# Low parts of the retention's weights made beside the first FFN's down products and loaded later; the heads' normalization as one scale and bias on ScalarE

## The chip, the cores and the metric

The kernel runs on one core of one Trainium2 chip. The metric is the device time of one execution in microseconds (us), as the median of several runs. A trace of one execution gives the times of the instructions. TensorE (PE), VectorE (DVE), ScalarE (ACT), GpSimd (POOL) and SyncE (SP) each work their own queue of instructions in order; SP here only issues DMAs, and ACT and POOL issue some beside their other work.

## The reference

One block of a streaming encoder on 1024 frames of 1024 channels in f32: half a SwiGLU FFN, two token mixers on the same normalized input, a gated merge, a second half FFN, a gated embedding and a last norm.

```
h = h + 0.5 * swiglu(rms_norm(h, ffn1_norm), ffn1_w_gate, ffn1_w_up, ffn1_w_down)
u = rms_norm(h, mix_norm)
z = u @ w_in                     # q, k, v of attention, indexer and retention, and gates
aq, ak, av, iq, ik, iw, rq, rk, rv, rg, ga, gb = split(z)
y_a = dsa_attention(...)         # an indexer selects 256 keys of each query
y_r = group_norm_heads(retention(rope(rq), rope(rk), rv)) * silu(rg)
merged = sigmoid(ga) * (y_a @ w_branch_a) + sigmoid(gb) * (y_r @ w_branch_b)
h = h + merged @ w_out
h = h + 0.5 * swiglu(rms_norm(h, ffn2_norm), ...)

def group_norm_heads(y, g):      # per frame and head, over the head's 256 values
    mean = mean(y); var = mean((y - mean) ** 2)
    return (y - mean) * rsqrt(var + GN_EPS) * g
```

Retention has 4 heads with q and k of 128 and v of 256 channels each.

## The kernel before, in words

Every matrix product is made of three products of rounded factors: each f32 operand is split into a high part and a low part, and high by high, low by high and high by low are summed. A weight tile is 128 x 1024 values. For each, SP loads the raw tile (`wraw`), ACT copies it into the rounded type (`wh`, L144), and DVE or POOL subtracts to get the low part (`wl`, L146). The class `Weights` keeps the list of all tiles in the order in which they are used; four raw buffers and some seven pairs of `wh` and `wl` go round, so that loads and splits run ahead of their use. Whether DVE or POOL subtracts is an argument of each tile, `side`: POOL does it for the gate tiles, for the retention's heads and for `aq`.

PE's order is written out by hand (a manual schedule); the order on the other engines, and that in SP's queue, is set by the framework's scheduler from the program's text and its own costs. A semaphore between engines is waited for where a tile is shared.

The stages that matter here, by the trace:

- The first FFN's gate and up products end at about 503 us. Its weights are combined into seven products of the Strassen-Winograd kind, by POOL and DVE.
- The down products, 503 to 719 us: seven runs (A11, A12, S2, S1, S3, S4, A22, in this order), each over the same loop of 11 weight tiles (`NJ2`). A tile is 4 x 3 products of 128x512 with its own left and right half as factors (L683); half of a tile's values is an activation that POOL spilled before (`hf`), half is the weight. Only the last run has work between its tiles (`between`: the norm and the transposes of the mixers' input).
- Small products, the indexer's products and its scores, 719 to 880 us.
- The retention, some 880 to 1326 us: 32 units, one for each head and block of 128 frames. The weights of a head are four tiles `("r", h)`, 16 in all, and the gates' tiles are used in between (16 x 3 products of a gate tile into `pgate`, L1058, ACT then writes `gt`, L1065, which goes to DRAM, `gspill`). In a unit: q, k and v products (`prod`), the rope, the scores, the state's update (`sf`, `sh`, `sl`), the cross part (`y`, L1256, on ACT), then in `ret_values` the sum of both parts and the normalization (`bs`, `mv`, `y`, L1264 to L1274), and the transposed result times the gate.
- Through the first 19 or so of these units the attention's selection runs beside on DVE and ACT: 31 times, six blocks are compared with a candidate. For four of them DVE writes a mask (`bias`, L1124, 1024, 896, 768 and 640 columns) and ACT sums it (L1125), for two DVE does both (`eq`, L1127); then `hit`, `thr`, `cand`.
- Attention follows to 1548 us, the merge to 1710, and the second FFN, which is like the first.

Of the kernel before, what the change touches and what calls it, by code (L numbers as in the profile page):

```python
# [20 lines left out]
P = 128  # L21
# [67 lines left out]
class Weights:  # L89
# [3 lines left out]
    def __init__(self, nc):  # L93
        self.nc = nc
        self.raw_free, self.free, self.half_open = [], [], None
        self.loads, self.fills, self.pair, self.rows = [], [], {}, {}
        self.loaded = self.filled = 0
        self.limit = 0
        self.dropped = []

    def add(self, pool, raws=0, pairs=0):
        t = [pool.tile([P, 1024], F32, name=f"wraw{i}") for i in range(raws)]
# [45 lines left out]
    def plain(self, key, k, c, side, pieces):  # L148

        n = k * c  # L150

        def load(t):
            v = t[:, :n].rearrange("p (k c) -> p k c", k=k)
            for c0, c1, ap in pieces:
                self.nc.sync.dma_start(v[:, :, c0:c1], ap)

        at = self.new_load(1, load)

        def fill(slot, _):
            self.split(slot.h[:, :n], slot.l[:, :n], self.raw(at)[:, :n], side)  # L160
            self.used(at)
            return [(key, tuple(x[:, :n].rearrange("p (k c) -> p k c", k=k) for x in (slot.h, slot.l)))]

        self.fills.append(([at], False, 1, fill))
        self.rows[key] = k

    def matrix(self, key, top, bottom):

# [109 lines left out]
def hybrid_block_kernel(  # L278
# [14 lines left out]
    def krows(w, c0, c1, k0, k1):  # L293
        return w.rearrange("(k p) c -> p k c", p=P)[:, k0:k1, c0:c1]
# [55 lines left out]
    AQ, AK, IQ, IK, RQ, RK, RV, RG, GA, GB = 0, 512, 640, 1152, 1224, 1736, 2248, 3272, 4296, 5320  # L350
    TILES = [(RG, f) for f in range(8)] + [(c, f) for f in range(8) for c in (GB, GA)]

    def gate_jobs(n0, n1):
        for c, f in TILES[n0:n1]:
            c0 = c + f * P
            W.plain((c, f), KT, P, True, [(0, P, krows(w_in0, c0, c0 + P, 0, KT))])

    for i in range(2):
        group_jobs(("pp", i), w_ple_proj[0], [(512 * i, 512 * i + 512)], nk=2)
# [4 lines left out]
    gate_jobs(0, at_tile)  # L364
    for h in range(RH):
        group_jobs(("r", h), w_in0, [(RQ + P * h, RQ + P * h + P), (RK + P * h, RK + P * h + P),
                                     (RV + 256 * h, RV + 256 * h + 256)], side=True)
        gate_jobs(at_tile, at_tile + N_RET[h])
        at_tile += N_RET[h]
    group_jobs("aq", w_in0, [(AQ, AQ + 512)], side=True)  # L370
    gate_jobs(at_tile, len(TILES))
# [17 lines left out]
    def tok(b):  # L389
        return slice(b * P, (b + 1) * P)  # L390
# [93 lines left out]
    class Seven:  # L484
# [175 lines left out]
                gp.dma_start(wsp[self.name][j][:, :, 256 * q:256 * q + 256],  # L660
                             wd[q].rearrange("p f i c -> p (f i) c"))

        def down(self, hres, residual, finished, turn, other={}):
            bank_plan(mm=3, m1=1, dn=4)
            sums = [bank(t, "pda") for t in ("mm", "mm", "mm", "m1")]

# [8 lines left out]
            def run(a, ps, start, stop, between=None, load=None):  # L675
                for j in range(NJ2):
                    key = self.name, a, j
                    h, l = (x[:, 0] for x in W[key])
                    if load and j == 4:
                        load(h)  # L680
                    for i in range(4):
                        for n, (x_, y_) in enumerate(split3(h[:, tok(i)], l[:, tok(i)], h[:, 512:D], l[:, 512:D])):
                            nc.tensor.matmul(ps[i], x_, y_, start=start and j == 0 and n == 0,  # L683
                                             stop=stop and j == NJ2 - 1 and n == 2, skip_group_check=True)
                    W.release(key)
                    if between and between.get(j):
                        between[j]()

# [193 lines left out]
            f()  # L882

    finished = normed(mix_norm[0], hres, hspill)
    seven.down(hres, lambda b, i: x0[tok(b), half(i)], finished, turn, {4: lambda: W.drop(raws)})
    for b in range(2):
        for j in range(2):
            sm_product(2 * b + j, "dn")
# [369 lines left out]
    def ret_values(n):  # L1258
# [12 lines left out]
        nc.vector.bn_aggr(mv[:, 0:2], bs)  # L1271
        nc.vector.tensor_scalar(mv[:, 2:3], mv[:, 1:2], GN_EPS, None, op0=OP.add)
        nc.gpsimd.tensor_tensor(mv[:, 3:4], mv[:, 2:3], mhalf, op=OP.pow)
        nc.vector.tensor_scalar(y, y, mv[:, 0:1], mv[:, 3:4], op0=OP.subtract, op1=OP.mult)  # L1274
        R[n, "z"] = y

    def ret_store(n):
# [396 lines left out]
```

## Time and profile before

| | |
|---|---|
| median of 3 runs | 2575.51 us (2575.15 to 2577.4) |
| the profiled execution | 2573.51 us |
| its span in the trace | 2571.7 us |
| PE busy | 2467.5 us (96% of the span) |
| DVE busy | 1619.0 us (63%) |
| ACT busy | 1104.6 us (43%) |
| POOL busy | 1011.3 us (39%) |
| PE's granted clock, mean of the span | 0.986 |
| DMA | 349.34 MB, mean 136 GB/s |

The span is the time from the first to the last instruction of the trace; the profiled execution's own time is 1.8 us more. Busy times of different engines overlap. The clock is in shares of PE's full speed.

### The profile page before, as it was taken

The page shows a single profiled execution, that of the slowest core. Times are in us where ns is not written, and L with a number is a line of the kernel's source. Part 1 is how long each engine was busy: PE and PEld are TensorE (multiplying, and loading weights), DVE is VectorE, ACT ScalarE, POOL GpSimd, SP SyncE. Part 2 cuts the span into 40 slices and gives each one's busy share as a digit, 9 for nine tenths or more (in the row PEclk, how much of TensorE's full clock was granted, in tenths as well). Part 3 has the DMA queues.
Part 4 walks back from the last instruction along what each step waited for, and adds up shares of the span by engine and source line. Part 5 has one row for each costly group of instructions (what it writes and reads, how often), then busy time and mean ns, then how long its engine had stood idle before and what let it go on. Part 6 is the DMA issues. An engine that isn't in the chain of part 4 may idle for free.

```text
span 2571.7 us, 32603 instructions
## 1 busy us (share of the span) xinstructions
PE 2467.5 (96%) x11464; PEld 2016.4 (78%) x11464; DVE 1619.0 (63%) x2640; ACT 1104.6 (43%) x1900; POOL 1011.3 (39%) x934
## 2 busy tenths in 40 slices
PE   6999999999999989889999999999899999999998
PEld 5788877878887877667878887787688788878887
DVE  5555556575667889997457774644556665555564
ACT  5333333343445666652245663423433333333442
POOL 5667668400011343343343431003676686520000
PEclk9999999999999999999999999999999999999999
DMA  6345444586621222222221227653254444587622
GB/s 204 121 141 172 156 143 164 178 272 210 217 83 35 77 62 59 59 72 60 72 82 38 77 64 223 190 168 103 90 172 156 144 164 145 175 278 225 193 94 95
DMA packets 262052, 349.34 MB, mean 136 GB/s; under 512 B 20864, under 2 KB 172672, under 8 KB 259072
## 3 DMA queue, kind: packets, MB, share of 16 engines
q1 hardware_dynamic: 239264, 267.03, 34.2%
q0 software_dynamic: 15712, 67.64, 6.8%
q10 hardware_dynamic: 6912, 12.59, 1.3%
q8 instruction: 90, 1.47, 0.2%
q14 instruction: 74, 0.61, 0.1%
HBM read 246.00 MB, written 101.19 MB: 135 GB/s over the span
## 4 chain that ended last, share of the span: by engine, by line
PE 72%; DVE 13%; issue 5%; ACT 4%; POOL 3%; DMA 3%; SPq 0%; ACTq 0%; POOLq 0%; DVEq 0%
PE pa L566 18%; PE pc L566 13%; PE prod L440 10%; PE pda L683 9%; PE pdc L683 7%; PE pgate L1058 5%; PE pmrg L396 4%; DVE bias L1124 3%; DVE wl L146 1%; ACT bias L1125 1%; PE psc L396 1%; PE ppv L1388 1%; PE ppt L1377 1%; PE plg L396 1%; ACT wh L144 1%
## 5 line engine op out<-in xcount | busy, mean ns | idle before, releaser
L146 DVE TENSOR_TENSOR wl<-wraw,wh 128x1024 fp32r<-128x1024 f32 (+2 forms) x422 | 621.6, 1476 | 406.6 <-ACT wh L144 402.1
L144 ACT ACTIVATE wh<-wraw 128x1024 fp32r<-128x1024 f32 (+1 forms) x466 | 435.9, 937 | 759.4 <-PE pc L566 184.3
L440 PE MATMUL prod<-wh,uh 128*128 128x512 f32 (+1 forms) x648 | 266.0, 411 | 0.2 <-ACT gt L1065 0.2
L440 PE MATMUL prod<-wh,ul 128*128 128x512 f32 (+1 forms) x648 | 256.8, 396 | 0.0
L440 PE MATMUL prod<-wl,uh 128*128 128x512 f32 (+1 forms) x648 | 256.4, 396 | 0.0
L1058 PE MATMUL pgate<-uh,wh 128*128 128x512 f32 x384 | 158.9, 414 | 23.2 <-ACT gt L1065 22.3
L1058 PE MATMUL pgate<-uh,wl 128*128 128x512 f32 x384 | 153.8, 401 | 0.0
L1058 PE MATMUL pgate<-ul,wh 128*128 128x512 f32 x384 | 153.7, 400 | 0.0
L440 PEld LDWEIGHTS prod<-wh,ul 128*128 128x128 f32 x648 | 123.1, 190 | 29.0
L146 POOL TENSOR_TENSOR wl<-wraw,wh 128x1024 fp32r<-128x1024 f32 x44 | 108.9, 2478 | 91.5 <-ACT wh L144 91.0
L566 PE MATMUL pa<-uh,wh 128*128 128x512 f32 x352 | 141.2, 401 | 2.5 <-DVE ev L581 2.5
L1125 ACT ACTIVATE bias<-bias 128x1024 bf16<-128x1024 bf16 (+3 forms) x132 | 117.1, 888 | 59.0 <-DVE bias L1124 55.1
L683 PE MATMUL pda<-wh 128*128 128x512 f32 x352 | 138.7, 394 | 3.8 <-ACT wh L144 3.8
L566 PE MATMUL pa<-ul,wh 128*128 128x512 f32 x352 | 139.9, 398 | 1.5 <-DVE ul L403 1.5
L566 PE MATMUL pa<-uh,wl 128*128 128x512 f32 x352 | 139.7, 397 | 0.0
L566 PE MATMUL pc<-uh,wl 128*128 128x512 f32 x352 | 139.4, 396 | 0.0
L566 PE MATMUL pc<-ul,wh 128*128 128x512 f32 x352 | 139.3, 396 | 0.0
L683 PE MATMUL pda<-wl,wh 128*128 128x512 f32 x352 | 137.8, 391 | 1.5 <-DVE wl L146 1.5
L566 PE MATMUL pa<-th,wl 128*128 128x512 f32 x352 | 139.2, 395 | 0.0
L566 PE MATMUL pc<-uh,wh 128*128 128x512 f32 x352 | 139.2, 395 | 0.0
L566 PE MATMUL pa<-tl,wh 128*128 128x512 f32 x352 | 138.9, 395 | 0.0
L440 PEld LDWEIGHTS prod<-wh,uh 128*128 128x128 f32 x648 | 124.1, 191 | 18.5 <-ACT gt L1065 0.4
(280 smaller groups left out, 6000.6 us busy)
## 6 DMA issues: line engine op xcount, KB each, us to landing
wraw<-hf SPq DMA_DIRECT2D x154, 256.0 KB, 3.3
wraw<-in_ffn_w_gate_dram SPq DMA_DIRECT2D x44, 512.0 KB, 4.0
wraw<-in_ffn_w_up_dram SPq DMA_DIRECT2D x44, 512.0 KB, 3.9
wd<-in_ffn_w_down_dram SPq DMA_DIRECT2D x88, 256.0 KB, 4.3
wf<-wd POOLq DMA_DIRECT2D x44, 512.0 KB, 3.3
hf<-g POOLq DMA_DIRECT2D x22, 1024.0 KB, 5.6
wraw<-wf SPq DMA_DIRECT2D x88, 256.0 KB, 3.7
wraw<-in_ffn_w_down_dram SPq DMA_DIRECT2D x66, 256.0 KB, 3.9
```

The costliest lines, as they stand in the source:

```text
L144: self.nc.scalar.activation(h, src, AF.Copy)
L146: eng.tensor_tensor(l, src, h.bitcast(F32), op=OP.subtract)
L396: nc.tensor.matmul(ps, a, b, start=i == 0, stop=i == n - 1)
L440: nc.tensor.matmul(box[0][:, :cols], a, w, start=k == 0 and i == 0, stop=k == nk - 1 and i == 2)
L566: nc.tensor.matmul(ps, x_, y_, start=start and k == 0 and i == 0, stop=stop and k == 3 and i == 2, skip_group_check=True)
L683: nc.tensor.matmul(ps[i], x_, y_, start=start and j == 0 and n == 0, stop=stop and j == NJ2 - 1 and n == 2, skip_group_check=True)
L1058: nc.tensor.matmul(box[0], a, m, start=k == 0 and j == 0, stop=k == KT - 1 and j == 2)
L1124: nc.vector.tensor_scalar(m, x_, t[:, j:j + 1], None, op0=op)
L1125: nc.scalar.activation(m, m, AF.Copy, accum_out=cnt[:, j:j + 1])
L1377: nc.tensor.transpose(ps[:, (t - t0) * P:(t - t0 + 1) * P], L[:, t * P:(t + 1) * P], ident)
L1388: nc.tensor.matmul(pv[:, j].rearrange("p a c -> p (a c)"), vhl[:, s], pT[:, t].rearrange("p a c -> p (a c)"), start=s == 0, stop=s == b)
```

## The change

Two things are changed.

1. For 24 weight tiles (the 16 of the retention's heads and the 8 gate tiles that are used among them) the low part is made in the first FFN's down stage. `Weights.make`, called after tiles 1, 3, 5, 7 and 9 of each run that has nothing else between its tiles, loads up to three of these tiles ahead by SP into `lraw` (three buffers), makes the high part on ACT (`lh`), subtracts on POOL in place, and has POOL's queue write the result to DRAM (`low`). With five calls to a run, the 24 calls fall in A11, A12, S2, S1 and S3. In the retention ACT makes `wh` as before, and `wl` is loaded by a DMA on ACT's queue from `low`; POOL's subtraction of these 24 tiles is gone. The first gate tiles, `aq` and the later gates are as before.
2. In `ret_values`, y times `mv[3]` plus (minus mean times `mv[3]`) on ACT takes the place of DVE's subtraction and multiplication, with one more one-column operation on DVE for the bias.

```diff
--- before.py
+++ after.py
@@ -97,6 +97,23 @@
         self.loaded = self.filled = 0
         self.limit = 0
         self.dropped = []
+        self.to_make, self.making, self.made = [], [], {}
+
+    def make(self, pool, dram):
+
+        while self.to_make and len(self.making) < 3:
+            key, load = self.to_make.pop(0)
+            raw = pool.tile([P, 1024], F32, name="lraw", tag="lraw", bufs=3)
+            load(raw)
+            self.making.append((key, raw))
+        if not self.making:
+            return
+        key, raw = self.making.pop(0)
+        h = pool.tile([P, 1024], F32R, name="lh", tag="lh", bufs=2)
+        self.nc.scalar.activation(h, raw, AF.Copy)
+        self.nc.gpsimd.tensor_tensor(raw.bitcast(F32R), raw, h.bitcast(F32), op=OP.subtract)
+        self.made[key] = dram.tile([P, 1024], F32, name=f"low{len(self.made)}")
+        self.nc.gpsimd.dma_start(self.made[key], raw)
 
     def add(self, pool, raws=0, pairs=0):
         t = [pool.tile([P, 1024], F32, name=f"wraw{i}") for i in range(raws)]
@@ -157,12 +174,18 @@
         at = self.new_load(1, load)
 
         def fill(slot, _):
-            self.split(slot.h[:, :n], slot.l[:, :n], self.raw(at)[:, :n], side)
+            if side == "made":
+                self.nc.scalar.activation(slot.h, self.raw(at), AF.Copy)
+                self.nc.scalar.dma_start(slot.l.bitcast(F32), self.made[key])
+            else:
+                self.split(slot.h[:, :n], slot.l[:, :n], self.raw(at)[:, :n], side)
             self.used(at)
             return [(key, tuple(x[:, :n].rearrange("p (k c) -> p k c", k=k) for x in (slot.h, slot.l)))]
 
         self.fills.append(([at], False, 1, fill))
         self.rows[key] = k
+        if side == "made":
+            self.to_make.append((key, load))
 
     def matrix(self, key, top, bottom):
 
@@ -350,10 +373,10 @@
     AQ, AK, IQ, IK, RQ, RK, RV, RG, GA, GB = 0, 512, 640, 1152, 1224, 1736, 2248, 3272, 4296, 5320
     TILES = [(RG, f) for f in range(8)] + [(c, f) for f in range(8) for c in (GB, GA)]
 
-    def gate_jobs(n0, n1):
+    def gate_jobs(n0, n1, side=True):
         for c, f in TILES[n0:n1]:
             c0 = c + f * P
-            W.plain((c, f), KT, P, True, [(0, P, krows(w_in0, c0, c0 + P, 0, KT))])
+            W.plain((c, f), KT, P, side, [(0, P, krows(w_in0, c0, c0 + P, 0, KT))])
 
     for i in range(2):
         group_jobs(("pp", i), w_ple_proj[0], [(512 * i, 512 * i + 512)], nk=2)
@@ -364,8 +387,8 @@
     gate_jobs(0, at_tile)
     for h in range(RH):
         group_jobs(("r", h), w_in0, [(RQ + P * h, RQ + P * h + P), (RK + P * h, RK + P * h + P),
-                                     (RV + 256 * h, RV + 256 * h + 256)], side=True)
-        gate_jobs(at_tile, at_tile + N_RET[h])
+                                     (RV + 256 * h, RV + 256 * h + 256)], side="made")
+        gate_jobs(at_tile, at_tile + N_RET[h], "made")
         at_tile += N_RET[h]
     group_jobs("aq", w_in0, [(AQ, AQ + 512)], side=True)
     gate_jobs(at_tile, len(TILES))
@@ -660,7 +683,7 @@
                 gp.dma_start(wsp[self.name][j][:, :, 256 * q:256 * q + 256],
                              wd[q].rearrange("p f i c -> p (f i) c"))
 
-        def down(self, hres, residual, finished, turn, other={}):
+        def down(self, hres, residual, finished, turn, other={}, beside=lambda: None):
             bank_plan(mm=3, m1=1, dn=4)
             sums = [bank(t, "pda") for t in ("mm", "mm", "mm", "m1")]
 
@@ -683,6 +706,8 @@
                             nc.tensor.matmul(ps[i], x_, y_, start=start and j == 0 and n == 0,
                                              stop=stop and j == NJ2 - 1 and n == 2, skip_group_check=True)
                     W.release(key)
+                    if j % 2 and not between:
+                        beside()
                     if between and between.get(j):
                         between[j]()
 
@@ -882,7 +907,8 @@
             f()
 
     finished = normed(mix_norm[0], hres, hspill)
-    seven.down(hres, lambda b, i: x0[tok(b), half(i)], finished, turn, {4: lambda: W.drop(raws)})
+    seven.down(hres, lambda b, i: x0[tok(b), half(i)], finished, turn, {4: lambda: W.drop(raws)},
+               lambda: W.make(rt_pool, dram))
     for b in range(2):
         for j in range(2):
             sm_product(2 * b + j, "dn")
@@ -1271,7 +1297,8 @@
         nc.vector.bn_aggr(mv[:, 0:2], bs)
         nc.vector.tensor_scalar(mv[:, 2:3], mv[:, 1:2], GN_EPS, None, op0=OP.add)
         nc.gpsimd.tensor_tensor(mv[:, 3:4], mv[:, 2:3], mhalf, op=OP.pow)
-        nc.vector.tensor_scalar(y, y, mv[:, 0:1], mv[:, 3:4], op0=OP.subtract, op1=OP.mult)
+        nc.vector.scalar_tensor_tensor(mv[:, 2:3], mv[:, 0:1], -1.0, mv[:, 3:4], op0=OP.mult, op1=OP.mult)
+        nc.scalar.activation(y, y, AF.Identity, bias=mv[:, 2:3], scale=mv[:, 3:4])
         R[n, "z"] = y
 
     def ret_store(n):
```

POOL's queue in the first FFN's down products. `hres` are the tiny copies that a run makes at its tile 4, `hf` the last of the spilled activations; before:

```order
L635 DMA hf_85<-g_638 128x2048
L637 DMA hf_85<-s_3497 128x512
L671 COPY hres<-wh_3521 128x1 x4
L671 COPY hres<-wh_71 128x1 x4
L671 COPY hres<-wh_73 128x1 x4
L671 COPY hres<-wh_69 128x1 x4
L466 TENSOR_TENSOR nst<-nst,mhalf 128x1 x8
```

After, with the subtractions and writes (`lraw`, `low`) among them:

```order
L658 DMA hf_85<-g_638 128x2048
L660 DMA hf_85<-s_3497 128x512
L114 TENSOR_TENSOR lraw<-lraw,lh 128x1024 x2
L116 DMA low_3663<-lraw 128x1024
L116 DMA low_3704<-lraw 128x1024
L694 COPY hres<-wh_3521 128x1 x4
L114 TENSOR_TENSOR lraw<-lraw,lh 128x1024
L116 DMA low_3751<-lraw 128x1024
L114 TENSOR_TENSOR lraw<-lraw,lh 128x1024
L116 DMA low_3790<-lraw 128x1024
L694 COPY hres<-wh_71 128x1 x4
```

All 24 subtractions and their writes stand between the copies of the runs; the rows shown are those of the first two.

SP's queue for the first run, A11; `hf` is the activation half of a tile, `in_ffn_w_down` the weight half. Before:

```order
L155 DMA wraw_136<-hf_79 128x512
L155 DMA wraw_136<-in_ffn_w_down_dram 128x512
L155 DMA wraw_135<-hf_80 128x512
L155 DMA wraw_135<-in_ffn_w_down_dram 128x512
L155 DMA wraw_65<-hf_81 128x512
L155 DMA wraw_65<-in_ffn_w_down_dram 128x512
```

After, at the same tiles (in brackets the semaphores that a load waits for: DMAHW of DMAs on SP's queue, DMASW of DMAs on POOL's, DVE and Pool of those engines):

```order
L172 DMA wraw_136<-hf_79 128x512 [waits DMAHW1_49,DVE_49]
L172 DMA wraw_136<-in_ffn_w_down_dram 128x512 [waits DMAHW2_49]
L172 DMA lraw<-in_w_in_dram 128x8x128 [waits DMAHW3_49,DMASW0_49]
L172 DMA wraw_135<-hf_80 128x512 [waits DMAHW4_49,DVE_49]
L172 DMA wraw_135<-in_ffn_w_down_dram 128x512 [waits DMAHW5_49]
L172 DMA wraw_65<-hf_81 128x512 [waits DMAHW6_49,DVE_49]
L172 DMA wraw_65<-in_ffn_w_down_dram 128x512 [waits DMAHW7_49]
L172 DMA lraw<-in_w_in_dram 128x8x128 [waits DMAHW0_49,DMASW1_49,Pool_49]
L172 DMA wraw_66<-hf_82 128x512 [waits DMAHW1_49,DVE_49]
L172 DMA wraw_66<-in_ffn_w_down_dram 128x512 [waits DMAHW2_49]
```

The loads of `lraw` (one of 8 pieces of 128 columns for a gate tile, three for a tile of the heads) stand between the loads of the weights that follow, and wait for POOL's subtraction and for the write of the tile that had the buffer before. Ahead of the load of the last tile of S3 there are 22 tiles' worth of them.

ACT's queue at a head's change in the retention, before: `bias` are the sums of the selection, `wh` the high parts.

```order
L144 ACTIVATE wh_3523<-wraw_66 128x1024
L1125 ACTIVATE bias,cnt<-bias 128x1024
L144 ACTIVATE wh_69<-wraw_65 128x1024
L1125 ACTIVATE bias,cnt<-bias 128x896
L1125 ACTIVATE bias,cnt<-bias 128x768
L1223 ACTIVATE sts<-stf 128x128
L1125 ACTIVATE bias,cnt<-bias 128x640
L1242 ACTIVATE sh<-sf 128x256
L144 ACTIVATE wh_73<-wraw_66 128x1024
L1256 ACTIVATE y<-pc,cs 128x256
L402 ACTIVATE qkt<-pqkt 128x256
```

After, at the same unit; `wl` from `low` are the DMAs that ACT issues, and L1301 is the new activation.

```order
L179 DMA wl_3524<-low_3986 128x1024
L178 ACTIVATE wh_3523<-wraw_66 128x1024
L178 ACTIVATE wh_69<-wraw_65 128x1024
L1301 ACTIVATE y<-y,mv 128x256
L179 DMA wl_70<-low_4025 128x1024
L1249 ACTIVATE sts<-stf 128x128
L1268 ACTIVATE sh<-sf 128x256
L179 DMA wl_74<-low_4064 128x1024
L178 ACTIVATE wh_73<-wraw_66 128x1024
L1282 ACTIVATE y<-pc,cs 128x256
L425 ACTIVATE qkt<-pqkt 128x256
L1235 ACTIVATE kd<-qk,cs 128x128
```

The sums of the selection that stood among these rows stand elsewhere, each `wh` has a DMA beside it, the rows of `y` are new, and `kd` stands behind `qkt`. Over the whole, the selection had 9 of its iterations ahead of the first unit's rope and its last in unit 18 or so; it now has 7 and its last in unit 21.

## Rows read from the trace of the kernel before

**Rows 1.** Windows: stretch, then busy us (instructions) by engine, clock, DMA share, GB/s.

```profile
core 0: us, PE busy (x) PEld busy (x) DVE busy (x) ACT busy (x) POOL busy (x), PEclk, DMA share, GB/s
...
503.00:635.00 132.00, 129.48 (x570) 106.55 (x570) 83.91 (x102) 54.57 (x56) 14.42 (x23) 1.00 0.76 244
520.00:570.00 50.00, 50.00 (x222) 41.41 (x221) 40.76 (x64) 24.21 (x27) 2.29 (x8) 1.00 0.84 270
2270.00:2300.00 30.00, 30.00 (x133) 24.76 (x133) 18.96 (x18) 14.86 (x14) 1.60 (x4) 1.00 0.94 317
920.00:1200.00 280.00, 246.67 (x1130) 197.94 (x1129) 257.14 (x661) 160.35 (x365) 105.11 (x101) 0.93 0.20 59
1200.00:1326.00 126.00, 124.57 (x634) 103.43 (x634) 64.12 (x184) 41.15 (x87) 53.72 (x57) 1.00 0.29 83
```

**Rows 2.** Waits of PE, 720 to 1330 us: total, times, longest.

```profile
PE pgate L1058 <- ACT gt L1065: 22.3, 10, 4.7
```

**Rows 3.** The `bs` of the units: with the selection, and after it.

```profile
L1270 DVE BATCH_NORM_STATS2 bs<-y x18: 395/414/420, 965.2 to 1179.7; 128x6 f32<-128x256 f32 x18
...
L1270 DVE BATCH_NORM_STATS2 bs<-y x9: 414/419/428, 1242.9 to 1322.6; 128x6 f32<-128x256 f32 x9
```

**Rows 4.** Timelines of DVE, then of POOL, 1023 to 1037 us.

```profile
1023.82 2.49 DVE L1124 TENSOR_SCALAR bias<-sc,cand 128x896 bf16<-128x896 f32 x1
...
1028.89 2.38 DVE L1124 TENSOR_SCALAR bias<-sc,cand 128x640 bf16<-128x640 f32 x1
...
1033.10 0.41 DVE L1274 TENSOR_SCALAR y<-y,mv 128x256 f32<-128x256 f32 x1 [0.43 <-POOL mv L1273]
...
1034.12 1.54 DVE L1124 TENSOR_SCALAR bias<-sc,cand 128x1024 bf16<-128x1024 f32 x2
...
1035.91 1.07 DVE L1124 TENSOR_SCALAR bias<-sc,cand 128x768 bf16<-128x768 f32 x2
...
1023.17 2.67 POOL L146 TENSOR_TENSOR wl<-wraw,wh 128x1024 fp32r<-128x1024 f32 x1
...
1028.53 2.39 POOL L146 TENSOR_TENSOR wl<-wraw,wh 128x1024 fp32r<-128x1024 f32 x1
```

**Rows 5.** Groups of instructions, 920 to 1210 us: busy us, mean ns, idle before.

```profile
L1125 ACT ACTIVATE bias<-bias 128x768 bf16<-128x768 bf16 (+1 forms) x110 | 97.4, 886 | 45.5 <-DVE bias L1124 41.5 <-DVE mv L1271 3.4
L1124 DVE TENSOR_SCALAR bias<-sc,cand 128x1024 bf16<-128x1024 f32 (+1 forms) x108 | 92.6, 886 | 0.7
...
L146 POOL TENSOR_TENSOR wl<-wraw,wh 128x1024 fp32r<-128x1024 f32 x15 | 38.5, 2570 | 11.9 <-ACT wh L144 11.6
...
L1274 DVE TENSOR_SCALAR y<-y,mv 128x256 f32<-128x256 f32 x20 | 12.4, 619 | 9.4 <-POOL mv L1273 9.4
...
L1256 ACT ACTIVATE y<-pc,cs 128x256 f32<-128x256 f32 x18 | 8.3, 459 | 2.8 <-PE pc L396 2.8
...
L1272 DVE TENSOR_SCALAR mv<-mv 128x1 f32<-128x1 f32 x20 | 2.9, 144 | 0.0
```

**Rows 6.** Timelines of ACT and of PE at a gate product.

```profile
1040.39 0.58 ACT L1065 ACTIVATE gt<-pgate 128x512 f32<-128x512 f32 x1
...
1041.03 0.79 PE L1058 MATMUL pgate<-uh,wh 128*128 128x512 f32 x1 [4.71 <-ACT gt L1065]
```

**Rows 7.** The page's DMA issues: KB each, us to landing.

```profile
wf<-wd POOLq DMA_DIRECT2D x44, 512.0 KB, 3.3
```

**Rows 8.** DVE's groups by form, 60 to 500 us.

```profile
L146 DVE TENSOR_TENSOR wl<-wraw,wh 128x1024 fp32r<-128x1024 f32 x44 | 77.5, 1761 | 71.6 <-ACT wh L144 71.6
```

**Rows 9.** Timelines of SP's queue, DVE and PE at tile 54.

```profile
630.92 0.32 SPq L155 DMA_DIRECT2D wraw<-hf  x1
...
640.54 1.23 DVE L146 TENSOR_TENSOR wl<-wraw,wh 128x1024 fp32r<-128x1024 f32 x1 [1.50 <-ACT wh L144]
...
652.40 0.39 PE L683 MATMUL pda<-wl,wh 128*128 128x512 f32 x1
```

**Rows 10.** DMA of 503 to 635 us in 40 equal slices.

```profile
GB/s 153 220 348 271 299 281 280 181 252 395 245 264 379 125 237 281 315 255 291 274 330 274 220 212 166 182 204 227 263 254 334 233 222 166 169 186 225 194 179 179
```

## The prediction

> **What bounds the kernel now.** I read the busy times by stretch first [rows 1]. PE carries nearly the whole span, so only a stage in which PE waits can give much, and a stage in which it never waits can only lose; these rows show which is which. In the down products of the first FFN (503 to 635 us) PE works 129.5 of 132 us at a clock of 1.00: nothing to gain there. In the retention with the selection (920 to 1200 us) it works 246.7 of 280 us at a granted clock of 0.93, while DVE works 257.1 of 280, or 92%. After the selection (1200 to 1326 us) PE is back at 124.6 of 126 us and clock 1.00, with DVE half idle. So the stage that the change aims at is bound by DVE and by what waits for DVE, not by PE.
>
> The wait list of PE over 720 to 1330 us [rows 2] has as its largest entry the gate product waiting for ACT's `gt`: ten times, 22.3 us. ACT is 57% busy there; `gt` comes late because ACT works in order, and counts and casts that themselves wait for DVE stand ahead of it (ACT's `bias` sums waited 41.5 us for DVE's `bias`, in the first row of [rows 5]). The `bs`, one for each unit, give the pace [rows 3]: 965.2 to 1179.7 us in 17 steps, 12.62 us a unit, with the selection; 1242.9 to 1322.6 us in 8 steps, 9.96 us, without it.
>
> Why DVE is so full shows in its timeline beside POOL's [rows 4]. A count over 128x1024 takes 0.77 us (two in 1.54) when POOL does no subtraction. But `bias` of 128x896 took 2.49 us from 1023.82 and `bias` of 128x640 2.38 us from 1028.89; each lies on a POOL `wl` of 2.4 to 2.7 us (1023.17 and 1028.53). `bias` reads one tensor and is held for almost the whole of POOL's instruction.
>
> **The change, part by part.**
>
> *Removed from the retention: 24 POOL subtractions, 15 of them in 920 to 1210 us (38.5 us of POOL)* [rows 5]. POOL's own time is worth nothing, it waits most of the time. What counts is DVE's held time. 108 `bias` counts take 92.6 us, mean 886 ns. Undisturbed ones are 0.77 us for 1024 columns and 0.54 for 768 (two in 1.07); over the four sizes (mean 832 columns) that is about 0.6, and I take 0.65. The excess is 108 x 0.236 = 25.5 us. `y` has a mean of 619 ns against 0.41 undisturbed (1033.10): 20 x 0.21 = 4.2 us.
>
> *Moved from DVE to ACT: the normalization of a head.* DVE loses `y` (20 x 0.41 = 8.2 us) and gets a one-column operation, which by the other one-column operation on `mv` (144 ns) costs 20 x 0.144 = 2.9 us. ACT gets a 128x256 activation, which by its own `y` of that shape takes 459 ns, 20 x 0.46 = 9.2 us; it is 57% busy, and the place that the activation has ahead of `sts` delays that by half a microsecond, less than what the unit gains. Nothing is charged for it; were ACT full, it would be 9 us.
>
> DVE's saving in the stage is then 25.5 + 4.2 + 8.2 - 2.9 = 35 us in some 20 units. DVE is 92% busy, so I count 92% of it as time of the stage: **32 us**. The bounds: at most every unit runs at the free pace, 19 x 2.66 = 50 us; at least DVE's certain saving without the stalls, 20 x 0.619 - 2.9, about 10 us, if the blocked time lay beside other waits. In the order PE's gate products keep their place, and the ACT rows around `v` and `kd` move by a place or two, so I take the value nearest to the engine that is full.
>
> *Added to the retention: 24 loads of a low part from DRAM, issued by ACT.* An issue took SP 0.32 us (at 630.92 [rows 9]); by that 15 are 5 us of ACT's queue, which has 120 us of idle time. The load of a weight half waits for the same slot as ACT's `wh` does. 512 KB from POOL's queue lands 3.3 us after issue [rows 7], against ACT's `wh` and then POOL's `wl` of 2.6 us before, and the DMA is 20% busy in this stage: nothing.
>
> *Added to the down products: 24 tiles' worth of loading, splitting and writing.* ACT gets 24 `lh` copies, at the mean of its instructions there (54.57 us in 56) 1 us each, and is 54.6 of 132 us busy. POOL gets 24 x 2.5 and is 14.4 of 132 busy. Both hide it. DVE's `wl` of 128x1024 took 1.23 us at 640.54 [rows 9], and 1.76 on the mean in 60 to 500 us, beside POOL's work on the FFN [rows 8]; five POOL subtractions of 2.5 us a run of 30 us make POOL 42% busy, so perhaps 0.3 us on each of 11 tiles, 3 us of a run in which a tile's low part is ready 11 us ahead of its use (tile 54: DVE ends at 641.77, PE starts at about 652.4 [rows 9]). Only in the first run, where that lead is not yet built, do I charge **3 us** (0 to 6).
>
> The DMA is what has no slack. In 503 to 635 us the kernel moves 244 GB/s, in 132 us 32.2 MB, and the engines are 76% busy [rows 1]. In SP's queue 22 of the new loads stand ahead of the load of tile 54 (the last one of S3), which SP issues at 630.92 [rows 9]; the first three stand ahead of the first run's loads and can go before 503 us. With about 20 writes of low parts by then, 39 x 0.524 = 20.4 MB come on top: 52.7 MB. To be there in time the load must have landed ACT's and DVE's 2.3 us before PE's start, by about 650, so the 52.7 MB have 147.5 us, 357 GB/s. What rate is there? The best stretch that I found, 2270 to 2300 us, moves 317 GB/s at 94% DMA share; 520 to 570 us moves 270 at 84%; single slices of 3.3 us reach 395 [rows 1, 10]. At 317 the last byte comes at 503 + 166.2 = 669.2 us, **19 us late**. At 270 it is 698, 48 late; at 395 it is on time. I take 317: the stretch is long and near full. SP's wait for the low write of three tiles before (a loop of load, `lh`, subtraction 2.5 and a write, 3.3 + 1 + 2.5 + 3.3 or about 10 us at the landing time of [rows 7], in three turns of two tiles each, 16 us) does not bind unless the DMA does; if it does, the weight loads queued behind that wait on SP come late, and PE with them, which is the same 19 us and not one more.
>
> The Trainium skill's page "DMA: Bandwidth & Descriptors", section "Where 436 GB/s comes from", puts the limit of HBM for one core at about 358 GB/s. By that figure 52.7 MB take 147.2 us and the load is on time, and the sum would be 19 us less; no long stretch of this trace reaches it, and the 94% stretch, scaled to full, is at 337.
>
> The sum: -32 + 19 + 3 = **-10 us** on the profiled 2573.5 us, which is 2 us under the median of the runs, 2575.5. On the median's scale: **2565.5 us**.
>
> **The rivals.**
>
> *B, the transfers fit.* DMA packets of the added loads fill the gaps of a 76% busy stage, at the rate of the peak slices; then the delay is 0 and the time 2575.5 - 32 + 3 = 2546.5. For it: slices of 395 and 379 GB/s. Against it: none lasts longer than 3.3 us. The skill's 358 GB/s would give this time too.
>
> *C, the other side: the transfers become the bound of the down products.* The added loads come in pieces of 512 bytes and 1 KB, and writes share the engines. At the 270 GB/s of 520 to 570 us the tile comes 48 us late: 2575.5 - 32 + 48 + 3 = 2594.5. It decides below the rate at which the delay eats the gain of 29: 52.7 MB in 176.5 us, 299 GB/s. For it: 84% DMA share at 270 GB/s, so the share and the rate don't rise together. Against it: 94% at 317.
>
> *D, the stage keeps its pace.* PE waits there for ACT's `gt`, and ACT's order is fixed; if its head is a count that waits for another thing, DVE's freed time becomes idle time. The gain is then 10: 2575.5 - 10 + 22 = 2587.5. For it: `gt` at 1040.39 is followed by a PE that had stood 4.71 us [rows 6], and the wait list names ACT and not DVE. Against it: 41.5 of the 45.5 us that ACT's sums waited are DVE's.
>
> *E, nothing.* Gain and loss cancel within 5 us: 2575.5.
>
> **Chances and range.** Forecast .45 (its own range 2548 to 2582), B .20, C .15, D .15, E .05. What a measurement of this kernel can tell is about 0.2%, 5 us: faster is below 2570.4. Of the forecast's .45 I put .31 there, .10 within, .04 above; B is all faster; D .03 within and .12 slower; C slower; E within. Together faster .51, same .18, slower .31. The range 2544 to 2594 holds all of the forecast and E, half of B and of C, and most of D: .80.
>
> **What would show it.** The `bias` counts of 920 to 1200 us near 650 ns; units at about 11 us; the gate's wait for `gt` halved; the granted clock there above 0.93. In 503 to 720 us: DMA above 310 GB/s on the mean, and PE waits for `wh` in runs S1 to S3 of 10 to 30 us together, with the end of the last run 15 to 25 us later. I am wrong if the DMA in that stage shows 350 or more with no wait (B), or below 300 (C); and if the unit stays above 12 us with DVE under 85% busy (D).

## The result, and the profile after

The changed kernel takes 2560.35 us (median of 4 runs, 2557.34 to 2562.26) against 2575.33 in the runs beside it: the ratio is 0.9939, with an interval of 0.9925 to 0.9952, so it is 15 us faster. The span of the profiled execution went from 2571.7 to 2555.4 us. The forecast was 2565.5.

The same stretches of the changed kernel; columns are those of [rows 1]:

```profile
core 0: us, PE busy (x) PEld busy (x) DVE busy (x) ACT busy (x) POOL busy (x), PEclk, DMA share, GB/s
503.00:635.00 132.00, 123.40 (x526) 100.08 (x526) 89.34 (x89) 62.36 (x65) 66.06 (x58) 0.97 1.01 346
...
920.00:1200.00 280.00, 266.22 (x1291) 217.01 (x1291) 236.24 (x695) 184.44 (x414) 70.36 (x94) 0.99 0.32 99
```

The two stages went opposite ways. In the retention PE is busy for 266 us of 280 where it was 247, its granted clock is 0.99 where it was 0.93, and DVE has come down from 257 to 236 us. In the down products PE is busy for 6 us less of 132, and at a granted clock of 0.97 where it was 1.00: it does 526 products where it did 570. The DMA share is full.

The groups of 920 to 1210 us, the units' `bs`, and PE's longest wait in 720 to 1340 us, which answer to [rows 5], [rows 3] and [rows 2]:

```profile
L1151 ACT ACTIVATE bias<-bias 128x640 bf16<-128x640 bf16 (+1 forms) x117 | 103.3, 885 | 17.4 <-DVE bias L1150 17.0
L1150 DVE TENSOR_SCALAR bias<-sc,cand 128x1024 bf16<-128x1024 f32 (+1 forms) x116 | 73.7, 668 | 0.7
...
L1301 ACT ACTIVATE y<-y,mv 128x256 f32<-128x256 f32 x22 | 13.2, 602 | 39.3 <-DVE mv L1300 39.3
...
L1300 DVE SCALAR_TENSOR_TENSOR mv<-mv 128x1 f32<-128x1 f32 x22 | 3.5, 160 | 10.5 <-POOL mv L1299 10.5
```

```profile
L1296 DVE BATCH_NORM_STATS2 bs<-y x21: 397/414/428, 971.4 to 1195.4; 128x6 f32<-128x256 f32 x21
...
L1296 DVE BATCH_NORM_STATS2 bs<-y x11: 414/418/428, 1207.2 to 1303.9; 128x6 f32<-128x256 f32 x11
```

```profile
PE pgate L1084 <- ACT gt L1091: 10.7, 9, 2.2
```

A count takes 668 ns where it took 886; ACT's sums wait 17 us for DVE where they waited 41.5; a unit beside the selection takes 224.0/20 = 11.2 us where it took 12.6; PE's wait for `gt` has halved. The last `bs` comes at 1303.9 us, 18.7 earlier than before.

What the down products lost is seen in the length of the seven runs, from the first matrix product of each to that of the next (the last: to its last product), in us, worked out from the PE records of one profile of each kernel:

```
kernel                      A11   A12   S2    S1    S3    S4    A22   A12 to S4
before                      33.1  29.9  29.9  30.0  29.9  29.9  33.3  149.6
changed                     38.6  29.9  31.2  33.1  36.5  30.0  33.3  160.7
made, not used              37.4  30.0  34.0  32.2  36.4  30.0  33.5  162.6
 the DMAs alone             38.3  29.9  29.9  29.9  30.3  29.9  33.4  149.9
 no copy on ScalarE         37.4  33.9  30.0  31.6  33.0  30.0  33.3  158.5
 no subtraction on POOL     39.3  29.9  29.9  31.1  35.1  29.9  33.3  155.9
four a run                  38.4  29.9  34.5  37.5  44.1  29.9  33.3  175.9
spread                      37.2  29.9  41.4  36.8  40.0  31.5  33.3  179.6
four tiles ahead            44.3  29.9  31.9  35.9  34.4  29.9  33.3  162.0
```

The changed kernel loses 5.5 us in the first run and 11.1 in S2 to S3, starts the stage 1.8 us earlier, and so ends it 14.8 us later than before. From there to the last unit it gains 33.5 us; at the end 16.3 are left of the span.

Three more things can be worked out from the same records. PE's idle time is the time between its products; its time at half clock is that at the lower of its two levels, 1.2 in place of 2.4 GHz, of which half is lost work. The lead of a tile is the time from the end of its `wl` on DVE to the first product that reads it (mean of a run's 11 tiles, in us):

```
                            A11            A12 to S4      lead of wl in
kernel                      idle  half     idle  half     S2    S1    S3
before                      2.5   0.0      0.0   0.0      10.9  11.3  11.3
changed                     5.2   6.8      7.6   3.4      2.4   1.3   1.8
made, not used              5.2   6.8      7.8   6.8      1.9   1.9   1.8
 the DMAs alone             5.3   6.8      0.1   0.0      7.4   4.3   1.9
 no copy on ScalarE         5.3   6.8      5.0   3.4      3.4   1.4   0.9
 no subtraction on POOL     6.1   6.8      4.0   0.0      6.2   2.7   1.0
four a run                  5.4   6.8      15.1  17.1     2.1   2.3   1.5
spread                      4.2   6.8      18.8  13.7     1.9   1.4   0.5
DVE subtracts (4)           3.3   6.8      0.0   0.0      11.2  11.3  11.3
```

In the changed kernel the granted clock was 0.50 from 516.9 to 523.7 us, after PE had stood idle for 4.6 us at 512, and 0.51 from 639.8 to 643.2, after idle times of 0.8 and 2.1 us.

### The profile page after: what moved, and what is told of

Read it like the earlier page. It is cut to its first block, busy times and chain, and to the rows that moved or that the text cites. A ratio compares the mean times of both kernels' runs of the same rounds, so it can differ in the third digit from the quotient of the medians.

```text
span 2555.4 us, 32814 instructions
## 1 busy us (share of the span) xinstructions
PE 2461.7 (96%) x11464; PEld 2014.4 (79%) x11464; DVE 1579.1 (62%) x2640; ACT 1144.0 (45%) x1956; POOL 1016.4 (40%) x958
## 4 chain that ended last, share of the span: by engine, by line
PE 72%; DVE 11%; DMA 5%; issue 4%; ACT 4%; POOL 3%; SPq 0%; ACTq 0%; POOLq 0%; DVEq 0%
PE pa L589 19%; PE pc L589 14%; PE prod L463 10%; PE pgate L1084 7%; PE pda L706 6%; PE pmrg L419 5%; PE pdc L706 5%; DVE wl L163 2%; DVE bias L1150 1%; ACT bias L1151 1%; DMA wraw<-hf 1%; DMA wraw<-wf 1%; PE psc L419 1%; PE ppv L1415 1%; PE ppt L1404 1%
## 5 line engine op out<-in xcount | busy, mean ns | idle before, releaser
L161 ACT ACTIVATE wh<-wraw 128x1024 fp32r<-128x1024 f32 (+2 forms) x442 | 409.6, 930 | 709.7 <-PE pc L589 195.5
L1084 PE MATMUL pgate<-uh,wh 128*128 128x512 f32 x384 | 156.7, 408 | 11.6 <-ACT gt L1091 10.7
L706 PE MATMUL pda<-wh,wl 128*128 128x512 f32 x352 | 139.4, 396 | 0.0
L589 PE MATMUL pa<-th,wh 128*128 128x512 f32 x352 | 137.9, 392 | 0.0
```

The source lines that it names most:

```text
L161: self.nc.scalar.activation(h, src, AF.Copy)
L589: nc.tensor.matmul(ps, x_, y_, start=start and k == 0 and i == 0, stop=stop and k == 3 and i == 2, skip_group_check=True)
L1084: nc.tensor.matmul(box[0], a, m, start=k == 0 and j == 0, stop=k == KT - 1 and j == 2)
```

## The experiments

**1. The normalization alone.** The kernel before, with the second part of the change only.

```diff
-        nc.vector.tensor_scalar(y, y, mv[:, 0:1], mv[:, 3:4], op0=OP.subtract, op1=OP.mult)
+        nc.vector.scalar_tensor_tensor(mv[:, 2:3], mv[:, 0:1], -1.0, mv[:, 3:4], op0=OP.mult, op1=OP.mult)
+        nc.scalar.activation(y, y, AF.Identity, bias=mv[:, 2:3], scale=mv[:, 3:4])
```

> Only the normalization is moved to ScalarE; no low part is made early. Theory (DVE's held time under POOL's subtractions is most of the gain, the moved operation a fifth): 4 to 8 us faster than the kernel before, the bias counts of 920 to 1200 us still near 880 ns, the down products unchanged. Rival (the moved operation is the gain, the stalls are not): 25 to 31 us faster, nearly the whole gain of the retention. Rival (neither on the path alone): within 2 us.

Measured: ratio 0.9992 (0.9983 to 1.0002), 2 us and not to be told from none, under the 4 to 8 of the theory. The counts take 781 ns on the mean, not near 880: of their excess over the changed kernel's 668 about half is still there. That counts shorter by 105 ns gave so little time is not explained. The moved operation is worth less than I gave it.

**2. The low parts alone.** The changed kernel with the line of `y` as before.

> The low parts are made in the down products and loaded in the retention, the normalization stays on DVE. Theory: the retention gains 23 to 28 us, the down products lose 15 us, together 8 to 13 us faster than before; bias counts near 670 ns. Rival (the moved operation is the gain): 12 to 15 us slower, the loss of the down products alone.

Measured: 0.9950 (0.9937 to 0.9962), 13 us faster; counts at 683 ns. With the 2 us of the first experiment that is the 15 of the whole change. The gain comes with the removal of POOL's subtractions from beside the selection.

**3. The low parts made and not used.** As 2, but the retention's tiles take POOL's subtraction again.

```diff
-            if side == "made":
-                self.nc.scalar.activation(slot.h, self.raw(at), AF.Copy)
-                self.nc.scalar.dma_start(slot.l.bitcast(F32), self.made[key])
-            else:
-                self.split(...)
+            self.split(slot.h[:, :n], slot.l[:, :n], self.raw(at)[:, :n], side)
```

> The low parts are made and written in the down products, but nobody reads them: the retention's are subtracted on POOL as before, and the normalization stays on DVE. Theory (the cost lies in the down products): 13 to 17 us slower than before, all of it between 503 and 735 us, and the retention as before. Rival (the run of changes after the first down stage shifts the scheduler's order and the loss lies elsewhere): within 5 us.

Measured: 1.0063 (1.0051 to 1.0076), 16 us slower; the runs from A12 to S4 lose 13.0 us, in the changed kernel 11.1, and the stage behind them is as long as before (604.6 us to the last unit, 603.4 before). So the making costs 16 us and what it makes is worth 29 (from 1.0063 to 0.9950).

**4. DVE subtracts.** The kernel before with the moved normalization, and `side=False` for the 16 tiles of the heads and the 8 gate tiles among them: nothing is made early.

> No low part is made early; the 24 subtractions in the retention are done by DVE itself in place of POOL, and the normalization is on ScalarE. Theory (POOL's subtraction holds DVE longer than DVE needs for it): DVE saves 35 us of held and moved time and gets 15 subtractions of 1.2 to 1.3 us, 19 us, so about 16 us less, 10 to 18 us faster, with the down products unchanged. Rival (DVE is the bound and each subtraction on it counts in full beside a stall that was partly hidden): 0 to 10 us slower.

Measured: 0.9903 (0.9890 to 0.9917), 25 us faster, more than the whole change, and more than the 10 to 18 us of the theory. The rows of 920 to 1210 us:

```profile
L1124 DVE TENSOR_SCALAR bias<-sc,cand 128x1024 bf16<-128x1024 f32 (+1 forms) x108 | 71.6, 694 | 0.7
...
L146 DVE TENSOR_TENSOR wl<-wraw,wh 128x1024 fp32r<-128x1024 f32 x20 | 26.2, 1308 | 3.3 <-ACT wh L144 3.0
```

DVE pays 1.31 us for a subtraction and is no longer held 2.5 us by POOL's; the counts, 694 ns, are nearly as short as in the changed kernel, and the down products run as before (29.9 to 30.0 us a run from A12 to S4). The theory's price, DVE's own time, is too small: from the end of the down products to the last unit DVE is busy for 14.5 us less, and the stage is 26.0 us shorter.

**5. The DMAs of the making alone.** As 3, but the tile is written out as it was loaded: no copy on ScalarE, no subtraction on POOL.

```diff
-        self.nc.scalar.activation(h, raw, AF.Copy)
-        self.nc.gpsimd.tensor_tensor(raw.bitcast(F32R), raw, h.bitcast(F32), op=OP.subtract)
```

> As the run with the low parts made and not used, but without the copy on ScalarE and the subtraction on POOL: the raw tile is loaded and written out as it is, so only the DMAs of the making are left. Theory (bandwidth is the cost): 10 to 16 us slower than before. Rival (POOL's subtraction holds DVE's own subtractions, 1.25 to 1.54 us each, and that makes the weights late): 0 to 5 us slower.

Measured: 1.0018 (1.0010 to 1.0027), 4.6 us slower, and the theory that bandwidth alone is the cost has fallen: from A12 on the runs lose 0.3 us together. Its windows, 540 to 635 us, with the columns of [rows 1]:

```profile
540.00:570.00 30.00, 30.00 (x134) 24.82 (x134) 18.99 (x25) 11.59 (x13) 3.20 (x9) 1.00 1.06 370
570.00:600.00 30.00, 30.00 (x134) 24.86 (x133) 15.78 (x15) 11.67 (x11) 4.19 (x9) 1.00 1.06 369
600.00:635.00 35.00, 35.00 (x156) 28.98 (x155) 15.72 (x15) 11.69 (x11) 3.18 (x9) 1.00 1.04 370
```

370 GB/s for almost a hundred microseconds, and PE without a wait. Only the first run loses, where PE waits once, 4.8 us. But the transfers are not free. The weights come later and later: in 535 to 690 us ScalarE waits 72.7 us for their loads, where it waited 5.4 before, and the lead of a tile's `wl`, 11.3 us in S3 before, has fallen to 1.9 us there, with 0.06 at the least. The transfers alone use up the lead that would cover a delay of an engine.

**6. The engines' part of the making alone.** As 3, without the DMAs: POOL sets the raw tile to a constant, nothing is written out.

```diff
-            load(raw)
+            self.nc.gpsimd.memset(raw, 0.5)
...
-        self.made[key] = dram.tile([P, 1024], F32, name=f"low{len(self.made)}")
-        self.nc.gpsimd.dma_start(self.made[key], raw)
```

> As the run with the low parts made and not used, but without its DMAs: a constant stands in the raw tile (set by POOL), ScalarE copies it and POOL subtracts, and nothing is written out. Theory (bandwidth is the cost): 0 to 4 us slower than before. Rival (POOL holding DVE is the cost): 10 to 16 us slower.

Measured: 1.0170 (1.0157 to 1.0184), 43 us slower, beyond the rival. As a price it is of no use: with no load to wait for, POOL did the subtractions, and the constants before them, almost one behind the other from 497 us on, and the run A12 took 64.9 us. But it shows the hold. DVE's timeline, then POOL's:

```profile
533.98 1.21 DVE L161 TENSOR_TENSOR wl<-wraw,wh 128x1024 fp32r<-128x1024 f32 x1
535.11 2.55 DVE L860 TENSOR_SCALAR kk<-kk 128x384 f32<-128x384 f32 x1
537.59 3.42 DVE L161 TENSOR_TENSOR wl<-wraw,wh 128x1024 fp32r<-128x1024 f32 x1
...
534.84 5.09 POOL L114 TENSOR_TENSOR lraw<-lraw,lh 128x1024 fp32r<-128x1024 f32 x2
```

`wl` takes 3.42 us in place of 1.21.

**7 and 8. The same making at a lower rate.** First four a run in six runs; then, in the second part of the diff, three a run (in the first run two, none of them before its tile 4) and four behind the down products.

```diff
-                    if j % 2 and not between:
+                    if j % 2 and j < 9 and not between:
...
-                    if j % 2 and not between:
+                    if j in ((4, 7) if a == "A11" else (1, 4, 7)):
...
             sm_product(2 * b + j, "dn")
+            W.make(rt_pool, dram)
```

> The changed kernel with four low parts made in each of six runs instead of five in five. Theory (bandwidth): a run of 29.9 us wants 5.77 MB of its own, 1.05 of the residual in the first four runs, and 4 x 1.05 of the making, 368 GB/s where five want 403; S3 and S4 want 333. Against the 355 to 362 GB/s that the changed kernel reached, the lag falls from 15 us to some 7 to 10, so 5 to 8 us faster than the changed kernel, 20 to 24 faster than before. Rival (the cost is by the number of subtractions or tiles and not by the rate): as the changed kernel, 15 us faster than before.

> The changed kernel with the making spread out: three a run in all seven runs (two in the first, none before its fifth tile) and four behind them beside the small products. A run wants at most 333 GB/s, under what was reached. Theory (bandwidth): the down products lose 0 to 5 us, 25 to 31 us faster than before. Rival (the cost is by the number of subtractions): as the changed kernel, 15 us faster than before.

Measured: 1.0007 (0.9999 to 1.0016) and 1.0006 (0.9996 to 1.0017). Both expectations failed, and the wrong way: fewer a run cost 26 and 30 us from A12 to S4 where five cost 11, at 313 and 308 GB/s in 540 to 670 us. The cost does not follow the rate. Over half of what these two lose is PE's idle time, and a quarter to a third the half clock (17.1 and 13.7 us at half clock in A12 to S4, where the changed kernel has 3.4). ScalarE's timeline in the kernel with the spread making shows one cause of the waits:

```profile
577.23 1.06 ACT L113 ACTIVATE lh<-lraw 128x1024 fp32r<-128x1024 f32 x1 [7.53 <-DMA lraw<-in_w_in_dram]
578.19 3.88 ACT L161 ACTIVATE wh<-wraw 128x1024 fp32r<-128x1024 f32 x4
```

The copy `lh` of a made tile stands 7.53 us until its load has landed, and behind it in ScalarE's queue wait four copies of weights that PE is about to need; they then run in one piece. The wait lists of ScalarE, 535 to 690 us, of the changed kernel, of four a run and of the spread one:

```profile
ACT lh L113 <- DMA lraw<-in_w_in_dram: 43.9, 19, 4.9
```

```profile
ACT lh L113 <- DMA lraw<-in_w_in_dram: 58.2, 18, 8.4
```

```profile
ACT lh L113 <- DMA lraw<-in_w_in_dram: 58.7, 19, 7.5
```

ScalarE's queue is not the only one. SP's wait list of the spread kernel, 535 to 690 us, has two entries that the changed kernel's lacks:

```profile
SPq L172 <- DMA low<-lraw: 14.6, 6, 4.9
SPq L695 <- POOL hres L694: 6.8, 1, 6.8
```

SP waits for the writes of earlier low parts and, once, for POOL's `hres` copies, which stand behind a subtraction that waits for `lh`; the weight loads behind these wait too. The kernel with four a run has only 3.1 us of the first. Why its raw tiles land later than at five a run is open.

**9 and 10. One engine's part each.** As 3, but POOL subtracts a constant tile and ScalarE makes no copy (9); or ScalarE copies and POOL doesn't subtract (10). Loads and writes are all there.

```diff
-        self.nc.scalar.activation(h, raw, AF.Copy)
-        self.nc.gpsimd.tensor_tensor(raw.bitcast(F32R), raw, h.bitcast(F32), op=OP.subtract)
...
+        self.nc.gpsimd.tensor_tensor(raw.bitcast(F32R), raw, self.const.bitcast(F32), op=OP.subtract)
...
-        self.nc.gpsimd.tensor_tensor(raw.bitcast(F32R), raw, h.bitcast(F32), op=OP.subtract)
```

> As the run with the low parts made and not used, but without ScalarE's copy: POOL subtracts a constant tile from the raw one, so POOL's 24 subtractions and all DMAs stay and ScalarE has no part in the making. Theory 1 (ScalarE works in order, and its copy, which waits up to 5 us for the raw tile's load, stands ahead of copies of weights that are there): the down products lose only the first run's 5 us, 3 to 7 us slower than before. Theory 2 (POOL's subtraction holds DVE's, 1.54 us each in place of 1.25): the down products lose 13 to 17 us, as with everything in place.

> As the run with the low parts made and not used, but without POOL's subtraction: ScalarE copies the raw tile when it has landed, and POOL's queue writes the raw tile out. Theory 1 (the copy that waits for its load holds the copies behind it): the down products lose 10 to 17 us, most of it in the runs S2 to S3, 10 to 17 us slower than before. Theory 2 (POOL's subtraction holds DVE): 3 to 7 us slower, the first run's loss alone. If both have a part, both of these two runs lose less than the whole of 15 us behind the first run, and their sum tells the shares.

Measured: 1.0039 (1.0024 to 1.0054) and 1.0040 (1.0026 to 1.0054), 10 us each. Neither theory holds alone. Against the DMAs alone (4.6 us), POOL's subtraction adds 5.4 us and ScalarE's copy 5.7; together 11.1, and the whole making (16.2) lies 11.6 over the DMAs. By the intervals each of the two shares is known to some 4 us, so that both have a part is shown, and that they are equal is not. From A12 to S4 it is 8.9 and 6.3 us beside 13.0 for both, all on top of the transfers, which have used up the lead. In 9 the loss of A12 is POOL's hold passed on, by DVE's and ScalarE's timelines:

```profile
551.19 2.78 DVE L869 SCALAR_TENSOR_TENSOR ang<-kh,ang 128x384 f32<-128x384 f32 x1
...
554.49 0.54 DVE L869 SCALAR_TENSOR_TENSOR ang<-kk,ang 128x384 f32<-128x384 f32 x1
...
556.47 0.53 ACT L872 ACTIVATE rope_t<-ang 128x384 f32<-128x384 f32 x1 [7.23 <-DVE ang L871]
```

An operation of the rope's tables takes 2.78 us beside POOL's subtraction and 0.54 without; ScalarE waits 7.23 us for the last of them, with weight copies behind it.

**11. All of the middle part's subtractions on DVE.** As 4, with the other gate tiles and `aq` as well.

> As the run with the retention's subtractions on DVE (23.5 us faster than before), and the other gate tiles' and the tile of the attention's queries as well: POOL subtracts no weight in the middle part at all. Theory (POOL's subtraction of 2.5 us holds DVE longer than DVE's own 1.25): a further 2 to 6 us, since most of these tiles lie where DVE is not full. Rival: DVE is late for the gates that follow each other at the start and the end of the middle part, 0 to 5 us slower than that run.

Measured: 0.9891 (0.9876 to 0.9906), 28 us faster than before, 3 more than 4 and within both intervals. It is the best of these kernels, some 12 us ahead of the changed one.

**12. Four raw tiles ahead.**

```diff
-        while self.to_make and len(self.making) < 3:
+        while self.to_make and len(self.making) < 4:
...
-            raw = pool.tile([P, 1024], F32, name="lraw", tag="lraw", bufs=3)
+            raw = pool.tile([P, 1024], F32, name="lraw", tag="lraw", bufs=4)
...
-        h = pool.tile([P, 1024], F32R, name="lh", tag="lh", bufs=2)
+        h = pool.tile([P, 1024], F32R, name="lh", tag="lh", bufs=1)
```

> The changed kernel with four raw tiles ahead in place of three (and one buffer for the copy in place of two, which the memory wants). Theory 1 (the copy waits for its load): each load is issued one call, some 5 us, earlier, the copies' waits for loads of 44 us fall by half or more, and the down products lose 5 to 10 us in place of 15, 5 to 8 us faster than the changed kernel. Theory 2 (POOL holds DVE), or bandwidth: as the changed kernel within 2 us.

Measured: 0.9955 (0.9942 to 0.9968), no better than the changed kernel. The copies' waits for loads fell to 39.6 us only, not to half, so the test didn't bring about what it was to test; A12 to S4 still lose 12.4 us, and the first run, with one more tile's load ahead of its own, took 44.3 us, 13.7 of them at half clock. That the loads come no earlier because they stand in SP's queue behind weight loads that wait for a free buffer was only argued.

## Why the prediction came out right

**The gain of the retention: the size right, the price right only in part.** 32 us were forecast for it, with counts near 650 ns, units near 11 us, the wait for `gt` halved and a clock above 0.93. Measured: 33.5 us to the last unit and 31 to the end, 668 ns, 11.2 us, 22.3 to 10.7 us, and 0.99. Experiment 3 beside 2, and 4 by another way, show that it is the absent subtractions that give it. Within it, the share of the moved normalization was too high: 35 us of DVE's time held 4.2 + 8.2 - 2.9 us for `y`, and alone it brought 2 us. ACT's `y` takes 602 ns, not 459.

What the other runs do not bear out is the price, 92% of DVE's saved time. From the end of the down products to the last unit, in us, by PE's and DVE's records:

```
kernel                 length   PE idle   PE at half clock   DVE busy
before                 603.4    39.2      41.0               470.9
changed                569.9    20.2      6.8                429.2
normalization alone    598.9    35.7      41.0               460.6
low parts alone        573.9    23.2      6.8                437.8
made, not used         604.6    37.9      44.4               468.9
DVE subtracts          577.4    25.8      10.2               456.4
```

Where DVE subtracts, 14.5 us less of DVE's time go with a stage 26.0 us shorter; where only the normalization moves, 10.3 with 4.5. In PE's time the changed kernel gains 19 us of idle time and 34 us at half clock, which are 17 us of work. The prediction had the clock as a sign and not as a term of the sum, so that 32 came so near is in part luck. How much the clock gave by itself, beside the waits that it follows, no run separates.

**The loss of the down products: the size within 7 us, by luck, and the cause wrong.** Forecast 19 us for the DMA and 3 for DVE in the first run; measured 14.8 at the stage's end. Of the signs, the rate came (331 GB/s in 503 to 720 us); PE stands idle in S1 and S3 for 6.6 us and not 10 to 30, and mostly for DVE's `wl` and not for `wh`. The step that failed is the term of the DMA, its rate of 317 GB/s: the same transfers alone ran at 370 and cost PE no time behind the first run (5). At that rate the prediction's 52.7 MB take 142 us and are on time, and rival B with its 2546.5 us should have come true. The Trainium skill's page "DMA: Bandwidth & Descriptors", section "Where 436 GB/s comes from", with its limit of about 358 GB/s was nearer than the rows that I took; the 370 measured lies a little above it.

"The DMA is what has no slack" was right as far as it goes: on time meant just on time. But the lead (11.3 us: tile 54's first product with `wl` is at 653.08, the one at 652.40 is still the tile before) was then counted twice, as time in which the load may come late and as cover for the engines' delays. The transfers alone use it up (1.9 us in S3), so delays that I had put down as hidden came through:

- "Both hide it", of ScalarE and POOL, was read from their busy shares. ScalarE had the time, but works in order: its copy of a made tile waits for that tile's load (43.9 us in all) ahead of copies that could run. That is some 5.7 us of the 11.6.
- DVE's held subtractions, which I had at 0.3 us a tile and covered by the lead, are the other half. In the changed kernel both act together, by ScalarE's, POOL's and DVE's timelines, and PE's:

```profile
635.42 1.06 ACT L113 ACTIVATE lh<-lraw 128x1024 fp32r<-128x1024 f32 x1 [4.57 <-DMA lraw<-in_w_in_dram]
636.39 1.99 ACT L161 ACTIVATE wh<-wraw 128x1024 fp32r<-128x1024 f32 x2
...
636.57 2.35 POOL L114 TENSOR_TENSOR lraw<-lraw,lh 128x1024 fp32r<-128x1024 f32 x1 [3.31 <-ACT lh L113]
...
637.46 3.68 DVE L163 TENSOR_TENSOR wl<-wraw,wh 128x1024 fp32r<-128x1024 f32 x2 [3.99 <-ACT wh L161]
...
640.06 0.80 PE L706 MATMUL pda<-wl,wh 128*128 128x512 f32 x1 [2.09 <-DVE wl L163]
```

The copy that came 4.57 us late releases POOL first and DVE's `wl` 0.9 us later, so that POOL has begun when DVE wants to: two subtractions take 3.68 us in place of 2.4, and PE waits; behind this wait its clock is at half for 3.4 us. That the same delays would have cost nothing beside a lead of 11 us is argued: no run has them without the transfers and at the changed kernel's pace (6 is too fast).

The first run's loss of 5.5 us is there with the DMAs alone (38.3 us), but most of it is not the making's. It is 2.7 us more of idle time and some 3 us of work lost in 6.8 us at half clock, and kernels without any making have such a half clock too: the run took 35.2 us with the normalization alone (3.4 us at half clock) and 36.5 where DVE subtracts (6.8). The profile of the kernel before, at 33.1, has none. Beside 36.5 the changed kernel's first run loses 2 us.

Rivals C and D did not come: PE's waits for `gt` did fall, and the transfers ran above 300 GB/s.

## What to carry to other kernels

Where POOL's work holds DVE, try first to give it to DVE itself: at 1.31 us against a hold of 2.5 that was worth 25 us here, without the 16 us that making the values early cost. An engine's idle share says whether work fits, not whether it is hidden: work put into an in-order queue brings its own wait along, and everything behind it waits too. Before a stage is said to be short of bandwidth, run its transfers alone, and read from that run not only its time but how much of the lead is left: a lead can be spent once.

## What the runs showed of the hardware

The DMA engines moved 369 to 370 GB/s, reads and writes together, over stretches of 30 to 35 us at a share of 1.04 to 1.06, where the fullest of the stretches read from the kernel before had 317 at 0.94. A subtraction of POOL's of 2.4 us held operations of DVE with one tensor input (128x384: 2.55 us in 6, where one of that form beside no subtraction took 0.35 us in 9) as well as those with two (`wl` 3.42 in place of 1.21). For the latter the Trainium skill's page "SBUF — State Buffer", section "Who interferes with whom", says so: an operation of DVE with two inputs in SBUF contends with a GpSimd instruction that reads there. The clock of PE came back from 0.93 to 0.99 in the retention as PE's waits got shorter, with no other change to its work: from the end of the down products to the last unit it was at half, 1.2 in place of 2.4 GHz, for 41.0 us before and 6.8 after.
